# A transformer trunk on one core: 1 / rms broadcast by two transfers instead of matmuls in three stages, and two steps of the weight splitting moved

## The chip, the cores and the metric

The kernel runs on one core of a Trainium2 chip. The metric is the device time of one execution in microseconds. "Before" is the kernel as it stood, "after" the kernel with the change. A core has five engines with instruction queues of their own, which run in order: PE (TensorE, matmuls), DVE (VectorE), ACT (ScalarE), POOL (GpSimd) and SP (which here only issues transfers). PEld is the loading of weights into TensorE.

## The reference

Two layers over 256 tokens of width 1024, all in float32:

```python
for i in range(DEPTH):                                   # DEPTH = 2
    h = h + 0.5 * swiglu(rms_norm(h, ffn_norm[i, 0]), ffn_w_in[i, 0], ffn_w_out[i, 0])
    u = rms_norm(h, mix_norm[i])
    h = h + (mla_mixer(u, ...) if i == 0 else fox_mixer(u, ...))
    h = h + 0.5 * swiglu(rms_norm(h, ffn_norm[i, 1]), ffn_w_in[i, 1], ffn_w_out[i, 1])
    gate = jax.nn.sigmoid(rms_norm(h, ple_norm[i]) @ ple_w_gate[i])
    h = h + gate * (p[i] @ ple_w_proj[i])
return rms_norm(h, final_norm)

def rms_norm(x, g):  return x * lax.rsqrt(jnp.mean(x * x, axis=-1) + 1e-6) * g
def swiglu(x, w_in, w_out):
    gate, up = jnp.split(x @ w_in, 2, axis=-1)           # 1024 -> 2 x 2816
    return (jax.nn.silu(gate) * up) @ w_out
```

`mla_mixer` is low-rank attention with 8 heads and a rotary key, `fox_mixer` attention with 8 heads and a forget gate. There are four feed-forward stages; I call them first to fourth. The second and fourth follow MLA and FoX.

## The kernel before, in words

The activations stand transposed: 128 features on the partitions, 256 tokens along the free axis, in eight blocks (`state`, `hT`). Every float32 matmul is made of float32r parts: an operand is split into a high part and the rest. A weight block comes from memory as `raw` (SP's queue, four buffers), ScalarE writes its high part `whi` (line 101), VectorE the rest `wlo` (line 105), into one of seven pairs of buffers. `W.pump()` puts one `wlo`, and up to two `whi` ahead of it, into the queues at the place where it is called; `W.begin()` puts one `whi` alone. The order of the program text is the order of the queues (`manual_schedule`): no scheduler moves anything.

A `Norm` collects a stage's squares (`sq`, added up on GpSimd as `acc`). The gain is multiplied into the matmul operand at once, 1 / rms only into the results. For that `by_token` sums `acc` over the partitions with matmuls by a column of ones (`pst`), forms the mean `v` on VectorE and takes the power -0.5 on GpSimd: `rtok`, one number per token, tokens on the partitions. `by_column` turns it round: matmuls against the identity give `pb`, with token t's number in column t of every partition, and ScalarE copies it to `rb`.

A feed-forward stage runs over 22 column blocks c, each a `pg` (gate) and a `pu` (up) of eight blocks of k in a PSUM bank; seven banks rotate. Of each, VectorE makes `two` = bank times `rb` (line 341), GpSimd adds its halves to `gu`, ScalarE applies Silu, GpSimd multiplies to `hid`, ScalarE and VectorE split that into `hs`. The first `two` stands behind the second `pu` in the program, because `rb` is wanted there. Then eight output blocks `po` follow. The first stage is special: it starts with four banks (`first`), while its weights come in, and has its sums from ScalarE (`sums`).

In MLA's attention the program goes over heads h: `shares(h - 2)` (VectorE: `inv`, `pr` scaled), `turn` (TensorE `pt`, ScalarE `ptS`), `scores(h - 1)` (TensorE `psc`, VectorE `pr` and bias `nm`, ScalarE the exponentials with their sums `den`), `values` (TensorE `po`). The weights of the output projection `mla_o` are split on the way: at the heads in `MLA_HIGHS` a `whi`, in `MLA_LOWS` a `wlo`. The rotated queries `yz` go to `kqv` by transfers of SP's queue. FoX first computes v by tokens (`pv`, three column blocks of eight k), and needs `rb` only for the queries and keys after that.

Of the kernel before, what the change touches and what calls it, by code (L numbers as in the profile page):

```python
# [11 lines left out]
F32 = mybir.dt.float32  # L12
# [3 lines left out]
AF = mybir.ActivationFunctionType  # L16
# [3 lines left out]
P = 128  # L20
D = 1024
T = 256
# [22 lines left out]

MLA_FILLS = {(6, 1): 3, (7, 1): 4, (8, 0): 1, (8, 1): 5, (9, 0): 4, (9, 1): 3, (10, 0): 2, (10, 1): 2}

MLA_HIGHS, MLA_LOWS = (0, 1, 6, 7, 8), (0, 1, 3, 6, 7, 8)
FOX_FILLS = {(8, 0): 4, (8, 1): 7, (9, 0): 6, (9, 1): 5}

PI_IN = 3.1415925
# [93 lines left out]
def trunk(ctx, tc, xT, xt, pT, pos, freq, bf, lead0, lead1, ffn_in, ffn_out, w_down, w_uq, w_ukv, mla_o,  # L145
          fox_qk, fox_v, fox_o, ple_gate, ple_proj, ple_rows, gain_row, out):
    nc = tc.nc
# [3 lines left out]
    act = ctx.enter_context(tc.tile_pool(name="act", bufs=2))  # L151
    work = ctx.enter_context(tc.tile_pool(name="work", bufs=2))
    psum = ctx.enter_context(tc.tile_pool(name="psum", bufs=7, space=bass.MemoryType.PSUM))
    psm = ctx.enter_context(tc.tile_pool(name="psm", bufs=1, space=bass.MemoryType.PSUM))


# [63 lines left out]
    W = Weights(nc, wp, plan)  # L220
# [52 lines left out]
    class Norm:  # L273
# [50 lines left out]
        def by_column(self):  # L324
            pb = psm.tile([P, T], F32, name="pb", tag="small")
            for t in range(2):
                nc.tensor.matmul(pb[:, t * P:(t + 1) * P], self.rtok[:, t:t + 1].to_broadcast([P, P]), ident,
                                 start=True, stop=True)
            self.rb = work.tile([P, T], F32, name="rb", bufs=3)
            nc.scalar.activation(self.rb, pb, AF.Copy)  # L330
            self.rb2 = self.rb.rearrange("p (o t) -> p o t", o=1).to_broadcast([P, 2, T])


    def ffn(norm, nxt, then=None, first=None, meanwhile=None, later=None):
        hs = big.tile([P, KF, 2, T], F32R, name="hs", tag="big")
        meanwhile = meanwhile or iter(())
        gu, hid = {}, {}
# [32 lines left out]
        if first:  # L370
            waits.append((bank("pg"), bank("pu")))
            first([p for ps in waits for p in ps])
        else:
            blocks(waits[0], norm.pair)
            W.pump(2)
        at = len(waits)
        for c in range(at, KF):
            pg = bank("pg")
            block(pg, norm.pair)
            if c == at:  # L380
                if not first:
                    norm.by_token()
                W.pump()
            else:
                gate(c, pg)
            pu = bank("pu")
            block(pu, norm.pair)
            if c == at:
                norm.by_column()
                for x, ps in enumerate(waits):  # L390
                    gate(x, ps[0], x)
                    up(x, ps[1], 0)
                gate(c, pg)
            up(c, pu, c > at)
# [304 lines left out]
    def fox(norm, nxt):  # L699
# [50 lines left out]
        for c in range(3):  # L750
            pv = [bank("pv0", (P, FV)), bank("pv1", (P, FV))]
            for k in range(KD):
                if k % 3 == 0:
                    w, = W.get()
                a = (k % 3) * FV
                for t in range(2):
                    mm3(pv[t], [norm.pair[:, k, u, t * P:(t + 1) * P] for u in range(2)],
                        [u[:, a:a + FV] for u in w[1:]], k == 0, k == KD - 1)
                if (c, k) == (0, 5):
                    norm.by_token()  # L760
                elif (c, k) == (1, 0):
                    norm.by_column()
                elif (c, k) == (1, 4):
                    steps = gates()
                if steps:
                    next(steps, None)
                if k % 3 == 2 or k == KD - 1:
                    W.done(w)
                    W.pump()
                    if k == 2:  # L770
                        W.catch_up(5)
            b = 0 if c else H
            for t in range(2):
                r = norm.rtok[:, t:t + 1]
                if c == 0:
                    nc.scalar.activation(zt[:, t, :].rearrange("p (j i) -> p j i", i=32)[:, :, :H],
                                         pv[t][:, :H].rearrange("p (o h) -> p o h", o=1).to_broadcast([P, 3, H]),
                                         AF.Copy, scale=r)
                nc.scalar.activation(v[:, t, c * FV + b - H:(c + 1) * FV - H], pv[t][:, b:], AF.Copy, scale=r)
# [223 lines left out]
    def first(ps):  # L1003
# [6 lines left out]
        for k in range(1, KD):  # L1010
            if k % 2 == 0:
                w, = W.get()
            for i, p in enumerate(ps):
                part(p, w, n0.pair, range(k, k + 1), KD - 1, at=lambda x: (k % 2 * 4 + i) * P)
            if k % 2:
                W.done(w)
                W.pump()
            if k == 1:

                n0.sums = const.tile([P, 2], F32, name="sums")  # L1020
                for t in range(2):
                    nc.scalar.activation(tokens[:, t, :], tokens[:, t, :], AF.Square,
                                         accum_out=n0.sums[:, t:t + 1])
            if k == 5:
                n0.by_token()


# [114 lines left out]
    for i in range(2):  # L1142
# [8 lines left out]
        if i == 0:  # L1151
            n0, n1 = Norm(G_FFN + 16, KD, D), Norm(G_MIX + 8, KD, D)
            ple(p.pair, n3, n0)
            ffn(n0, n1, AF.Exp)
        else:
            ple_by_token(p.pair, n3)

# [83 lines left out]
```

## Time and profile before

| | |
|---|---|
| median of 3 runs | 995.11 us (994.88 to 996.27) |
| the profiled execution's own time | 997.11 us |
| its span from first to last instruction | 995.3 us |
| mean granted TensorE clock | 0.998 |
| DMA | 182.26 MB, 183 GB/s, 58.4% of 16 engines' span on SP's queue |

A row of the timeline is start, duration in us, engine, line, operation, output <- inputs and shape; in brackets the idle time before it and whose work ended it. A row with xN stands for N in a row. A row of a list of waits is "engine, tile, line <- engine, tile, line: us in total, times, longest". Places in the span: MLA from about 194 to 263 us, the second feed-forward stage from 264, FoX from about 668 to 771, the fourth feed-forward stage from 771.5.

### The profile page before, as it was taken

How to read it: one execution, taken by the hardware profiler on the slowest of the kernel's cores; microseconds unless marked ns; L12 is line 12 of the kernel's file. 1: busy time of each engine (PE TensorE's matmuls, PEld its weight loads, DVE VectorE, ACT ScalarE, POOL GpSimd, SP SyncE). 2: the span in 40 equal slices, each digit the busy share in tenths (PEclk: the TensorE clock that was granted, in tenths of full speed). 3: DMA queues.
4: the chain of work that ended last, by engine and by line, in shares of the span. 5: the costliest groups of instructions: out<-in, count | busy, mean ns of one | idle time of the engine just before them, and what ended most of it. 6: DMA issues, size and time to landing. Idle time of an engine off the chain costs nothing.

```text
span 995.3 us, 15921 instructions
## 1 busy us (share of the span) xinstructions
PE 984.1 (99%) x5850; PEld 869.3 (87%) x5850; DVE 741.2 (74%) x1089; ACT 515.3 (52%) x820; POOL 425.8 (43%) x348
## 2 busy tenths in 40 slices
PE   8999999999999999999999999999999999999996
PEld 7888888998988888889988888899889888888885
DVE  6777879677877887667878886666877778786664
ACT  7555544456555454545555544537445554444552
POOL 1777731110277765111477673211221577771110
PEclk9999999999999999999999999999999999999999
DMA  8676666563356666665466665656543566666561
GB/s 314 181 253 210 195 173 198 183 182 115 115 185 209 191 189 176 190 202 185 142 200 208 191 186 175 193 178 219 153 148 100 179 209 194 189 179 204 180 208 42
DMA packets 53405, 182.26 MB, mean 183 GB/s; under 512 B 6224, under 2 KB 7760, under 8 KB 53200
## 3 DMA queue, kind: packets, MB, share of 16 engines
q1 hardware_dynamic: 52752, 180.40, 58.4%
q8 instruction: 46, 0.75, 0.3%
q10 hardware_dynamic: 576, 0.85, 0.3%
q14 instruction: 31, 0.25, 0.1%
HBM read 179.00 MB, written 1.05 MB: 181 GB/s over the span
## 4 chain that ended last, share of the span: by engine, by line
PE 94%; DMA 2%; DVE 1%; ACT 1%; issue 1%; POOL 0%; SPq 0%; POOLq 0%; ACTq 0%; DVEq 0%
PE po L247 16%; PE pu L247 16%; PE pg L247 16%; PE po L248 8%; PE pu L248 8%; PE pg L248 8%; PE ps L247 5%; PE ps L248 2%; PE ps L234 2%; PE ps L233 2%; PE ps L232 2%; DMA raw<-in_ffn_in_dram 1%; PE pv L232 1%; PE pv L234 1%; PE pv L233 1%; DMA lead<-in_lead_dram 1%
## 5 line engine op out<-in xcount | busy, mean ns | idle before, releaser
L105 DVE TENSOR_TENSOR wlo<-raw,whi 128x1024 fp32r<-128x1024 f32 (+2 forms) x339 | 416.6, 1237 | 15.2 <-ACT whi L101 14.7
L101 ACT ACTIVATE whi<-raw 128x1024 fp32r<-128x1024 f32 (+2 forms) x339 | 335.3, 1022 | 26.5 <-DMA raw<-in_ffn_in_dram 14.2
L343 POOL TENSOR_TENSOR gu<-two 128x256 f32<-128x256 f32 x176 | 235.7, 1340 | 118.0 <-DVE two L341 108.5
L247 PE MATMUL pg<-u,whi 128*128 128x512 f32 x702 | 251.2, 395 | 0.4 <-ACT whi L997 0.4
L247 PE MATMUL pu<-u,whi 128*128 128x512 f32 x702 | 251.0, 395 | 0.0
L247 PE MATMUL po<-hs,whi 128*128 128x512 f32 x704 | 246.8, 394 | 0.0
L248 PE MATMUL pg<-u,wlo 128*128 128x256 f32 x702 | 197.0, 281 | 0.3 <-DVE wlo L228 0.3
L248 PE MATMUL po<-hs,wlo 128*128 128x256 f32 x704 | 197.2, 280 | 0.0
L248 PE MATMUL pu<-u,wlo 128*128 128x256 f32 x702 | 196.8, 280 | 0.0
L247 PEld LDWEIGHTS po<-hs,whi 128*128 128x128 f32 x704 | 132.2, 188 | 31.3
L247 PEld LDWEIGHTS pg<-u,whi 128*128 128x128 f32 x702 | 131.8, 188 | 31.5 <-ACT whi L997 0.7
L247 PEld LDWEIGHTS pu<-u,whi 128*128 128x128 f32 x702 | 131.8, 188 | 30.9
L248 PEld LDWEIGHTS pg<-u,wlo 128*128 128x128 f32 x702 | 132.1, 188 | 1.0 <-DVE wlo L228 1.0
L248 PEld LDWEIGHTS po<-hs,wlo 128*128 128x128 f32 x704 | 132.3, 188 | 0.0
L248 PEld LDWEIGHTS pu<-u,wlo 128*128 128x128 f32 x702 | 132.1, 188 | 0.0
L303 POOL TENSOR_TENSOR acc<-acc,sq 128x256 f32<-128x256 f32 x42 | 46.3, 1102 | 174.2 <-ACT sq L298 152.7
L224 ACT ACTIVATE hs<-hid 128x256 fp32r<-128x256 f32 x88 | 36.8, 418 | 143.6 <-POOL hid L361 141.5
L361 POOL TENSOR_TENSOR hid<-sg,gu 128x256 f32<-128x256 f32 x88 | 105.5, 1199 | 6.9
L228 DVE TENSOR_TENSOR hs<-hid,hs 128x256 fp32r<-128x256 f32 x88 | 63.4, 720 | 48.7 <-ACT hs L224 48.7
L341 DVE TENSOR_TENSOR two<-pg,rb 128x512 f32<-128x512 f32 x88 | 60.3, 685 | 47.9 <-PE pg L248 39.9
L287 ACT ACTIVATE u<-state 128x256 fp32r<-128x256 f32 x47 | 24.0, 510 | 123.5 <-DVE state L408 105.3
L355 ACT ACTIVATE sg<-gu 128x256 f32<-128x256 f32 x88 | 36.8, 418 | 79.3 <-POOL gu L343 79.3
(258 smaller groups left out, 1163.4 us busy)
## 6 DMA issues: line engine op xcount, KB each, us to landing
raw<-in_ffn_in_dram SPq DMA_DIRECT2D x172, 512.0 KB, 4.1
raw<-in_ffn_out_dram SPq DMA_DIRECT2D x64, 512.0 KB, 3.8
raw<-in_ffn_out_dram SPq DMA_DIRECT2D x32, 384.0 KB, 3.4
raw<-in_fox_qk_dram SPq DMA_DIRECT2D x16, 512.0 KB, 4.6
raw<-in_mla_o_dram SPq DMA_DIRECT2D x8, 512.0 KB, 4.7
raw<-in_ple_gate_dram SPq DMA_DIRECT2D x8, 512.0 KB, 4.9
raw<-in_fox_o_dram SPq DMA_DIRECT2D x8, 512.0 KB, 3.5
raw<-in_ple_rows_dram SPq DMA_DIRECT2D x8, 512.0 KB, 4.5
```

The source lines that it names most:

```text
L101: self.nc.scalar.activation(self.pairs[i][0][:, c], self.raws[i][:, c], AF.Copy)
L105: self.nc.vector.tensor_sub(lo[:, c], self.raws[i][:, c], hi[:, c].bitcast(F32))
L224: nc.scalar.activation(hi, src, AF.Copy)
L228: nc.vector.tensor_sub(lo, src, hi.bitcast(F32))
L232: nc.tensor.matmul(ps, w[0], x[0], start=first, stop=False)
L247: nc.tensor.matmul(ps, hi, x[:, k], start=k == 0, stop=False)
L248: nc.tensor.matmul(ps[:, 1, :], lo, x[:, k, 0, :], start=False, stop=k == last)
L303: nc.gpsimd.tensor_add(new, self.acc, sq)
L341: nc.vector.tensor_mul(two, ps, norm.rb2)
L343: nc.gpsimd.tensor_add(gu[c, i], two[:, 0, :], two[:, 1, :])
L355: nc.scalar.activation(sg, gu.pop((c, 0)), AF.Silu)
L361: nc.gpsimd.tensor_mul(hid[c], gu.pop((c, 0)), gu.pop((c, 1)))
```

## The change

In the second and fourth feed-forward stage (`soon=True`) and in FoX's projections, `by_column` is replaced by `spread`: a transfer from GpSimd's queue writes the 256 values of `rtok` to a row in memory (`row`), and a second one, which waits for the first, reads that row into all 128 partitions of `rb`. In the two feed-forward stages `by_token` moves from behind the second `pg` to behind the first `pg` and `pu`, with one `wlo` moved behind it. In the third stage nothing changes (`soon=False`). In the first, `by_token` comes one step of k earlier. In MLA one `whi` moves from head 1 to head 2 and one `wlo` from head 3 to head 2. The whole diff:

```diff
--- before.py
+++ after.py
@@ -45,7 +45,7 @@
 
 MLA_FILLS = {(6, 1): 3, (7, 1): 4, (8, 0): 1, (8, 1): 5, (9, 0): 4, (9, 1): 3, (10, 0): 2, (10, 1): 2}
 
-MLA_HIGHS, MLA_LOWS = (0, 1, 6, 7, 8), (0, 1, 3, 6, 7, 8)
+MLA_HIGHS, MLA_LOWS = (0, 2, 6, 7, 8), (0, 1, 2, 6, 7, 8)
 FOX_FILLS = {(8, 0): 4, (8, 1): 7, (9, 0): 6, (9, 1): 5}
 
 PI_IN = 3.1415925
@@ -151,6 +151,7 @@
     act = ctx.enter_context(tc.tile_pool(name="act", bufs=2))
     work = ctx.enter_context(tc.tile_pool(name="work", bufs=2))
     psum = ctx.enter_context(tc.tile_pool(name="psum", bufs=7, space=bass.MemoryType.PSUM))
+    dram = ctx.enter_context(tc.tile_pool(name="dram", bufs=1, space=bass.MemoryType.DRAM))
     psm = ctx.enter_context(tc.tile_pool(name="psm", bufs=1, space=bass.MemoryType.PSUM))
 
 
@@ -328,10 +329,21 @@
                                  start=True, stop=True)
             self.rb = work.tile([P, T], F32, name="rb", bufs=3)
             nc.scalar.activation(self.rb, pb, AF.Copy)
+            self.both()
+
+        def spread(self):
+
+            row = dram.tile([1, T], F32, name="row", bufs=4)
+            nc.gpsimd.dma_start(row.rearrange("o (t p) -> p (o t)", p=P), self.rtok)
+            self.rb = work.tile([P, T], F32, name="rb", bufs=3)
+            nc.gpsimd.dma_start(self.rb, row.to_broadcast([P, T]))
+            self.both()
+
+        def both(self):
             self.rb2 = self.rb.rearrange("p (o t) -> p o t", o=1).to_broadcast([P, 2, T])
 
 
-    def ffn(norm, nxt, then=None, first=None, meanwhile=None, later=None):
+    def ffn(norm, nxt, then=None, first=None, meanwhile=None, later=None, soon=True):
         hs = big.tile([P, KF, 2, T], F32R, name="hs", tag="big")
         meanwhile = meanwhile or iter(())
         gu, hid = {}, {}
@@ -372,13 +384,17 @@
             first([p for ps in waits for p in ps])
         else:
             blocks(waits[0], norm.pair)
-            W.pump(2)
+            W.pump()
+            if soon:
+                norm.by_token()
+                norm.spread()
+            W.pump()
         at = len(waits)
         for c in range(at, KF):
             pg = bank("pg")
             block(pg, norm.pair)
             if c == at:
-                if not first:
+                if not (first or soon):
                     norm.by_token()
                 W.pump()
             else:
@@ -386,7 +402,8 @@
             pu = bank("pu")
             block(pu, norm.pair)
             if c == at:
-                norm.by_column()
+                if first or not soon:
+                    norm.by_column()
                 for x, ps in enumerate(waits):
                     gate(x, ps[0], x)
                     up(x, ps[1], 0)
@@ -758,8 +775,8 @@
                         [u[:, a:a + FV] for u in w[1:]], k == 0, k == KD - 1)
                 if (c, k) == (0, 5):
                     norm.by_token()
-                elif (c, k) == (1, 0):
-                    norm.by_column()
+                elif (c, k) == (0, 7):
+                    norm.spread()
                 elif (c, k) == (1, 4):
                     steps = gates()
                 if steps:
@@ -1021,7 +1038,7 @@
                 for t in range(2):
                     nc.scalar.activation(tokens[:, t, :], tokens[:, t, :], AF.Square,
                                          accum_out=n0.sums[:, t:t + 1])
-            if k == 5:
+            if k == 4:
                 n0.by_token()
 
 
@@ -1151,7 +1168,7 @@
         if i == 0:
             n0, n1 = Norm(G_FFN + 16, KD, D), Norm(G_MIX + 8, KD, D)
             ple(p.pair, n3, n0)
-            ffn(n0, n1, AF.Exp)
+            ffn(n0, n1, AF.Exp, soon=False)
         else:
             ple_by_token(p.pair, n3)
```

VectorE where the second feed-forward stage begins. Before (`u` is the normed operand of the stage, its last block):

```order
L292 SCALAR_TENSOR_TENSOR u<-state,u 128x256
L105 TENSOR_TENSOR wlo<-raw,whi 128x1024 x4
L320 TENSOR_SCALAR v<-pst 128x2
L105 TENSOR_TENSOR wlo<-raw,whi 128x1024
L341 TENSOR_TENSOR two<-pg,rb 128x512
L341 TENSOR_TENSOR two<-pu,rb 128x512
L341 TENSOR_TENSOR two<-pg,rb 128x512
```

and after:

```order
L293 SCALAR_TENSOR_TENSOR u<-state,u 128x256
L105 TENSOR_TENSOR wlo<-raw,whi 128x1024 x3
L321 TENSOR_SCALAR v<-pst 128x2
L105 TENSOR_TENSOR wlo<-raw,whi 128x1024 x2
L353 TENSOR_TENSOR two<-pg,rb 128x512
L353 TENSOR_TENSOR two<-pu,rb 128x512
L353 TENSOR_TENSOR two<-pg,rb 128x512
```

`v` now stands behind three `wlo` and not four. The queue is the same in the fourth stage.

GpSimd at the same place, before:

```order
L322 TENSOR_TENSOR rtok<-v,mhalf 128x2 x2
L303 TENSOR_TENSOR acc<-sq 128x256
L303 TENSOR_TENSOR acc<-acc,sq 128x256 x6
L322 TENSOR_TENSOR rtok<-v,mhalf 128x2
L343 TENSOR_TENSOR gu<-two 128x256 x2
L361 TENSOR_TENSOR hid<-sg,gu 128x256
```

and after:

```order
L323 TENSOR_TENSOR rtok<-v,mhalf 128x2 x2
L304 TENSOR_TENSOR acc<-sq 128x256
L304 TENSOR_TENSOR acc<-acc,sq 128x256 x6
L323 TENSOR_TENSOR rtok<-v,mhalf 128x2
L337 DMA row<-rtok 128x2x1
L339 DMA rb<-row 128x256
L355 TENSOR_TENSOR gu<-two 128x256 x2
L373 TENSOR_TENSOR hid<-sg,gu 128x256
```

The two transfers stand between the power and the first addition, which needs `rb` through `two`.

ScalarE in MLA, where the softmax of the first heads begins (`kqv` holds queries, keys and values), before:

```order
L618 ACTIVATE kqv<-ps 128x512
L101 ACTIVATE whi<-raw 128x1024 x2
L454 ACTIVATE pr,den<-pr,nm,qscale 128x128
L455 ACTIVATE pr,den<-pr,nm,qscale 128x256
L618 ACTIVATE kqv<-ps 128x512
L454 ACTIVATE pr,den<-pr,nm,qscale 128x128
L455 ACTIVATE pr,den<-pr,nm,qscale 128x256
```

and after:

```order
L635 ACTIVATE kqv<-ps 128x512
L101 ACTIVATE whi<-raw 128x1024
L471 ACTIVATE pr,den<-pr,nm,qscale 128x128
L472 ACTIVATE pr,den<-pr,nm,qscale 128x256
L635 ACTIVATE kqv<-ps 128x512
L101 ACTIVATE whi<-raw 128x1024
L471 ACTIVATE pr,den<-pr,nm,qscale 128x128
```

One `whi` has moved behind the exponentials of head 0 and the copy of queries.

## Prediction

> **What bounds the kernel now.** I read the page's busy shares first, then who waited for whom on TensorE, then the timelines of the places that the change touches.
>
> ```profile
> PE 984.1 (99%) x5850; PEld 869.3 (87%) x5850; DVE 741.2 (74%) x1089; ACT 515.3 (52%) x820; POOL 425.8 (43%) x348
> PE pb L327 <- POOL rtok L322: 1.0, 1, 1.0
> PE pt L469 <- DVE pr L462: 0.5, 1, 0.5
> PE po L476 <- ACT ptS L471: 0.3, 1, 0.3
> ```
>
> The first row is the page's: TensorE is busy 984.1 of 995.3 us, so it is the bound, and no other engine is above 74%. The others are from the waits of PE (us in total, times, longest). Apart from waits of a few tenths at the very start, these three are all it ever waits for. So the time falls by what TensorE is spared, and by these waits if they go; it rises by any new wait on TensorE. Nothing else counts.
>
> **Part 1: the broadcast matmuls, three stages.** In the second and fourth feed-forward stage and in the FoX projections, `by_column` (matmuls `pb`, then a copy on ScalarE) goes. TensorE's timeline in the second feed-forward stage:
>
> ```profile
> 275.35 0.28 PE L248 MATMUL pu<-u,wlo 128*128 128x256 f32 x1
> 275.47 0.60 PE L327 MATMUL pb<-ident,rtok 128*128 128x128 f32 x4
> 275.83 0.48 PE L247 MATMUL pg<-u,whi 128*128 128x512 f32 x1
> ```
>
> Matmuls overlap, so the cost is from start to start: `pb` holds the stream from 275.47 to 275.83, 0.36 us. Three times that is 1.1 us off the bound engine. The `pst` matmuls move but stay. ScalarE loses a 0.39 us copy per stage, which the bound does not feel.
>
> **Part 2: the first stage, `by_token` one step earlier.**
>
> ```profile
> 18.06 0.19 ACT L1022 ACTIVATION_READ_ACCUMULATOR lead<-lead 128x1 f32 x1
> 21.00 1.22 DVE L105 TENSOR_TENSOR wlo<-raw,whi 128x1024 fp32r<-128x1024 f32 x1 [4.07 <-ACT whi L101]
> 22.14 0.16 DVE L320 TENSOR_SCALAR v<-sums 128x2 f32<-128x2 f32 x1
> 22.46 1.69 POOL L322 TENSOR_TENSOR rtok<-v,mhalf 128x2 f32<-128x2 f32 x1 [20.97 <-DVE v L320]
> 22.93 0.28 PE L248 MATMUL pu<-u,wlo 128*128 128x256 f32 x1
> 24.20 0.71 PE L327 MATMUL pb<-ident,rtok 128*128 128x128 f32 x4 [1.00 <-POOL rtok L322]
> 23.75 1.06 ACT L101 ACTIVATE whi<-raw 128x1024 fp32r<-128x1024 f32 x1 [0.19 <-DMA raw<-in_ffn_in_dram]
> 39.07 1.21 DVE L105 TENSOR_TENSOR wlo<-raw,whi 128x1024 fp32r<-128x1024 f32 x1
> 41.58 0.39 PE L247 MATMUL pg<-u,whi 128*128 128x512 f32 x1
> ```
>
> The sums are ready at 18.25, but `v` stands on VectorE behind a weight subtraction that waits for its data until 21.00. With `v` ahead of it the power ends near 20.2, long before TensorE wants `pb` at 23.05 (22.93 plus the 0.12 between starts). The idle time from 23.05 to 24.20, 1.15 us, goes. What is late next: the copy `rb` stays behind the `whi` that ends at 24.81 on ScalarE, so the scaled evacuations don't move, while TensorE is 1.15 earlier. The tightest weight behind them, by my pairing of the subtractions with the plan, is the one that ends at 40.28, wanted at 41.58 and then at 40.43: 0.15 to spare. I take 1.1, between 0 and 1.15.
>
> **Part 3: `MLA_HIGHS` and `MLA_LOWS`.** One `whi` and one `wlo` of w_o change places with softmax work.
>
> ```profile
> 219.11 0.16 DVE L446 SCALAR_TENSOR_TENSOR nm<-m,qscale 128x2 f32<-128x2 f32 x1
> 219.58 1.06 ACT L101 ACTIVATE whi<-raw 128x1024 fp32r<-128x1024 f32 x1 [0.87 <-DMA raw<-in_mla_o_dram]
> 219.79 1.22 DVE L105 TENSOR_TENSOR wlo<-raw,whi 128x1024 fp32r<-128x1024 f32 x1
> 221.73 0.17 DVE L461 RECIPROCAL inv<-den 128x2 f32<-128x2 f32 x1 [0.72 <-ACT pr L455]
> 222.36 0.30 PE L469 MATMUL pt<-ident,pr 128*128 128x128 f32 x1 [0.54 <-DVE pr L462]
> 224.47 0.17 DVE L461 RECIPROCAL inv<-den 128x2 f32<-128x2 f32 x1 [1.24 <-ACT pr L455]
> 226.48 1.21 DVE L105 TENSOR_TENSOR wlo<-raw,whi 128x1024 fp32r<-128x1024 f32 x1
> 231.39 0.48 PE L476 MATMUL po<-ptS,kqv 128*128 128x256 f32 x1 [0.27 <-ACT ptS L471]
> ```
>
> The exponentials of head 0 have their bias at 219.27 but stand behind a `whi` that waits for its transfer and ends at 220.6. With the `whi` behind them they start 1.2 us earlier; the reciprocal then starts when VectorE's `wlo` ends, 220.95 instead of 221.73, and 0.78 covers the 0.54 of `pt`. The `wlo` of 226.48 moves up into the gap of 1.24 us before 224.47, so heads 2 and 3 come up to 1.2 earlier, which covers the 0.27 of `po`. Its raw transfer is issued sooner and stands on SP's queue ahead of the last four rotary copies, which are not ready yet then. Bounds 0 and 0.81; I take 0.7.
>
> **Part 4: what the transfers cost.** In FoX `rtok` is there at 673.2 and VectorE first uses `rb` at 691.87: 18 us, ample for any price below. In the feed-forward stages it is tight:
>
> ```profile
> 671.54 1.63 POOL L322 TENSOR_TENSOR rtok<-v,mhalf 128x2 f32<-128x2 f32 x1 [3.41 <-DVE v L320]
> 691.87 0.69 DVE L787 TENSOR_TENSOR two<-ps,rb 128x512 f32<-128x512 f32 x1 [0.36 <-PE ps L248]
> 266.13 0.88 POOL L303 TENSOR_TENSOR acc<-acc,sq 128x256 f32<-128x256 f32 x1 [0.39 <-ACT sq L298]
> 266.32 5.17 DVE L105 TENSOR_TENSOR wlo<-raw,whi 128x1024 fp32r<-128x1024 f32 x4
> 269.29 0.28 PE L248 MATMUL pu<-u,wlo 128*128 128x256 f32 x1
> 272.99 1.67 POOL L322 TENSOR_TENSOR rtok<-v,mhalf 128x2 f32<-128x2 f32 x1 [5.98 <-DVE v L320]
> 276.53 0.69 DVE L341 TENSOR_TENSOR two<-pg,rb 128x512 f32<-128x512 f32 x1 [2.43 <-ACT rb L330]
> 286.07 1.21 DVE L105 TENSOR_TENSOR wlo<-raw,whi 128x1024 fp32r<-128x1024 f32 x1
> 289.92 0.39 PE L247 MATMUL pu<-u,whi 128*128 128x512 f32 x1
> 784.25 0.69 DVE L341 TENSOR_TENSOR two<-pg,rb 128x512 f32<-128x512 f32 x1 [2.38 <-ACT rb L330]
> 793.77 1.21 DVE L105 TENSOR_TENSOR wlo<-raw,whi 128x1024 fp32r<-128x1024 f32 x1
> 797.62 0.39 PE L247 MATMUL pu<-u,whi 128*128 128x512 f32 x1
> ```
>
> Start. The sum of squares ends at 267.0, before `pst` at 269.41, so TensorE doesn't wait for it. After three of the four `wlo` VectorE is at 270.2 and does `v`. In the row of before the power ended 2 us after its `v` began, so `rtok` is there near 272.1. The two transfers follow; call the time from there to the first `two` the chain.
>
> Deadline. While VectorE waits for `rb`, every later `wlo` stands behind it. By the pairing, the tightest is the one that ends at 287.28, 10.75 after the first `two`, wanted at 289.92 less the 0.36 of `pb`: 289.56. So `rb` may come by 278.7 (0.1 for the hand-over), 2.2 later than now: the chain may last 6.6 us. In the fourth stage the same sum (793.77 + 1.21 - 784.25 = 10.73; 797.26) gives 6.5. Beyond that TensorE idles in both stages by the excess. PSUM isn't the limit: three free banks last past 283.9.
>
> Price. Nothing in this trace uses GpSimd's queue. The nearest rows (KB each, us to landing):
>
> ```profile
> fr<-in_freq_dram SPq DMA_DIRECT2D x1, 0.5 KB, 3.2
> pos_i<-in_pos_dram SPq DMA_DIRECT2D x1, 128.0 KB, 4.2
> p_sb<-in_pT_dram ACTq DMA_DIRECT2D x2, 256.0 KB, 2.6
> out_dram<-fin SPq DMA_DIRECT2D x2, 256.0 KB, 2.4
> ```
>
> `fr` is 128 single words, like `row`'s 256; `pos_i` has exactly `rb`'s shape, but stood in SP's queue among weights; `p_sb` had a queue of its own while weights streamed, as `rb` will. I take 3.2 for `row`, 2.6 for `rb`, 0.1 for each of two waits: 6.0, no stall. Low end: 2.4 + 2.6 = 5.0. High end: 3.2 + 4.2, and for GpSimd's own work per transfer its slowest power, 1.7 each: 10.8.
>
> The Trainium skill, "DMA: Bandwidth & Descriptors", section "Anatomy of one DMA — SWDGE (gpsimd) path", prices a transfer from this queue at about 2.0 us plus bytes over 436 GB/s; by it the chain would be an estimated 4.3 us and there would be no stall. No run here shows it yet.
>
> Behind the transfers on GpSimd stand only the additions that need `rb` anyway. The weight stream is hardly touched: 129 KB per stage against 0.5 MB per weight.
>
> **The sum.** 1.1 + 1.1 + 0.7 + 0 = 2.9 us. The profiled span is 995.3 of its execution's 997.1 us; against it the sum gives a span of 992.4. The median of the runs is 995.1, so 992.2. What a measurement of this kernel can tell from no change is about 0.2%, 2.0 us.
>
> **Rivals.**
>
> (a) The chain is too long by a little. Between 7 and 9 us it eats (chain - 6.5) twice: at 8 us, 3.0 of the 2.9, and the time is 995.2. For it speaks that `row` is words of four bytes and that the landings above vary from 2.4 to 4.2.
>
> (b) Slower: GpSimd writes the description of 256 separate words slowly. Then `rb` is late in two stages and each further microsecond costs two. No gain is left at 8.0; slower beyond 0.2% begins at 9.0. At the high end of 10.8 it is 4.3 x 2 - 2.9 = +5.7: 1000.8. For it: the power, a tiny job, takes 1.7 us on this engine beside VectorE. Against: VectorE is idle during most of the chain, and the engine is otherwise free.
>
> A milder form is that VectorE locks GpSimd out: if descriptors had to wait for the last `wlo`, which ends near 272.7, the chain would grow by 0.6 to 6.6, costing 0.1 in all: 992.3. The Trainium skill, "SBUF — State Buffer", section "Who interferes with whom", says that a tensor-tensor operation with both inputs in SBUF holds off GpSimd's reads, but not, as it infers, descriptor generation.
>
> (c) Parts 2 and 3 don't arrive: other waits take over at the same places (0.15 to spare in part 2). With nothing of both it is 1.1 alone: 994.0.
>
> **How the numbers follow.** Forecast, chain up to 7: 0.62, times from 991.5 to 993.1. (a) 0.20, 993.1 to 997.1. (b) 0.11, above. (c) 0.07, 993.2 to 994.5. Faster by over 0.2% (below 993.1) is the forecast: 0.62; same is (a) and (c): 0.27; slower 0.11. The range is 991.4 to 996.0: it leaves out (b), the last quarter of (a), and little below.
>
> **What would show it.** The first feed-forward stage without the 1.0 wait of `pb`; no wait of `pt` and `po` on PE; 20 instead of 32 `pb` matmul passes; `two` starting near 278 in the second stage (less what came earlier); PE without waits on `wlo` at the fourth `pu`. Such a wait near 288 and 795, with `two` waiting for the transfer of `rb`, proves me wrong.

## The result and the profile after

After takes 1009.63 us (median of 4 runs, 1009.17 to 1010.53), before, timed beside it, 995.37 (994.88 to 996.27). The ratio is 1.0142, 95% interval 1.0129 to 1.0154: 1.4% slower. The forecast was 992.2, in a range of 991.4 to 996.0.

The profiled execution of after took 1010.53 us, with a span of 1008.8. First the busy shares from its page, then the longest waits of PE behind the very start (us in total, times, longest):

```profile
PE 987.4 (98%) x5838; PEld 871.4 (86%) x5838; DVE 735.6 (73%) x1089; ACT 514.5 (51%) x817; POOL 427.9 (42%) x354
```

```profile
PE pu L248 <- DVE two L353: 7.8, 2, 4.5
PE pu L249 <- DVE wlo L105: 3.7, 2, 2.0
PE pst L318 <- POOL acc L304: 0.8, 1, 0.8
```

The waits of `pb` and `pt` are gone. In their place stand two pairs of new ones, 11.5 us together, one pair in each of the two feed-forward stages. The wait of `pst` (0.8) lies near 973 and also came up in `i_forms2` below, which is before with unread transfers, so the change does not explain it. The timelines of GpSimd, VectorE and TensorE in the second stage, one after the other, and then in the fourth:

```profile
267.78 1.61 POOL L323 TENSOR_TENSOR rtok<-v,mhalf 128x2 f32<-128x2 f32 x1 [3.50 <-DVE v L321]
269.70 0.90 POOL L337 DMA_DIRECT2D row<-rtok  x1 [0.31 <-POOL rtok L323]
280.38 0.59 POOL L339 DMA_DIRECT2D rb<-row  x1 [9.78 <-DMA row<-rtok]
283.60 0.69 DVE L353 TENSOR_TENSOR two<-pg,rb 128x512 f32<-128x512 f32 x1 [12.27 <-DMA rb<-row]
284.44 0.48 PE L248 MATMUL pu<-u,whi 128*128 128x512 f32 x1 [3.21 <-DVE two L353]
286.93 0.58 PE L249 MATMUL pu<-u,wlo 128*128 128x256 f32 x1 [2.01 <-DVE wlo L105]
...
782.38 1.63 POOL L323 TENSOR_TENSOR rtok<-v,mhalf 128x2 f32<-128x2 f32 x1 [3.50 <-DVE v L321]
784.30 0.74 POOL L337 DMA_DIRECT2D row<-rtok  x1 [0.29 <-POOL rtok L323]
794.98 0.57 POOL L339 DMA_DIRECT2D rb<-row  x1 [9.94 <-DMA row<-rtok]
799.56 0.69 DVE L353 TENSOR_TENSOR two<-pg,rb 128x512 f32<-128x512 f32 x1 [13.69 <-DMA rb<-row]
800.40 0.77 PE L248 MATMUL pu<-u,whi 128*128 128x512 f32 x1 [4.55 <-DVE two L353]
802.89 0.58 PE L249 MATMUL pu<-u,wlo 128*128 128x256 f32 x1 [1.73 <-DVE wlo L105]
```

Read it down. The power ends at 269.39 and the first `two` starts at 283.60: the chain lasts 14.2 us, not 6.0. Of it 10.4 us lie between the issue of `row` and its landing; GpSimd itself is occupied for only 0.90. In the fourth stage the chain is 15.6 us. At 281.2 the banks of PSUM are used up, and TensorE stands until the first `two` has freed one; soon after it stands again, for a `wlo` that is behind the late `two` on VectorE.

The list of DMA issues (KB each, median us to landing):

```profile
row<-rtok POOLq DMA_DIRECT2D x3, 1.0 KB, 10.4
rb<-row POOLq DMA_DIRECT2D x3, 128.0 KB, 4.5
```

So 1 KB takes over three times the 3.2 us of `fr`, the row from which it was priced. And the idle time is not all. Windows of 4 us (busy time by engine, then the granted clock, the DMA share, GB/s):

```profile
280.00:284.00 4.00, 1.23 (x8) 0.82 (x6) 0.40 (x1) 0.00 (x0) 0.59 (x1) 1.00 0.16 33
284.00:288.00 4.00, 1.55 (x5) 1.17 (x6) 2.93 (x5) 1.78 (x3) 3.55 (x4) 0.60 0.05 6
288.00:292.00 4.00, 4.00 (x15) 3.37 (x15) 2.99 (x4) 1.75 (x3) 2.89 (x4) 0.55 0.36 125
292.00:296.00 4.00, 4.00 (x25) 3.50 (x24) 3.94 (x5) 2.35 (x4) 2.90 (x3) 1.00 0.56 162
```

After the wait the granted clock is near one half in the two windows: TensorE is busy for all of 288 to 292 and issues 15 matmuls, against 25 in the next window. The trace's record of the clock has 0.5 for 6.83 us here, from 284.8, and again in the fourth stage from 800.2; before had no such stretch before its last microseconds. The Trainium skill, "TensorE: Matmul & The Clock Gate", section "Part 1: The HAM clock gate (the "warmup" mystery)", says that the array falls to half its clock after an idle window of about 3.4 us. The trace agrees roughly: of the 3.41 us ahead of the two stretches TensorE stood idle for 3.08 and for all; `m_quads` below shows that 2.15 can be enough.

### The profile page after: what moved, and what is told of

Read it like the earlier page. It is cut to its first block, busy times and chain, and to the rows that moved or that the text cites. A ratio compares the mean times of both kernels' runs of the same rounds, so it can differ in the third digit from the quotient of the medians.

```text
span 1008.8 us, 15918 instructions
## 1 busy us (share of the span) xinstructions
PE 987.4 (98%) x5838; PEld 871.4 (86%) x5838; DVE 735.6 (73%) x1089; ACT 514.5 (51%) x817; POOL 427.9 (42%) x354
## 4 chain that ended last, share of the span: by engine, by line
PE 90%; DVE 4%; DMA 3%; issue 1%; ACT 1%; POOL 1%; POOLq 0%; SPq 0%; DVEq 0%; ACTq 0%
PE po L248 16%; PE pu L248 15%; PE pg L248 15%; PE po L249 8%; PE pu L249 8%; PE pg L249 8%; PE ps L248 4%; PE ps L249 2%; DMA row<-rtok 2%; PE ps L233 2%; PE ps L234 2%; PE ps L235 2%; DVE wlo L105 1%; DVE state L534 1%; DMA rb<-row 1%
## 5 line engine op out<-in xcount | busy, mean ns | idle before, releaser
L355 POOL TENSOR_TENSOR gu<-two 128x256 f32<-128x256 f32 x176 | 225.8, 1284 | 120.6 <-DVE two L353 110.9
L248 PE MATMUL pu<-u,whi 128*128 128x512 f32 x702 | 254.9, 399 | 7.8 <-DVE two L353 7.8
L249 PE MATMUL pu<-u,wlo 128*128 128x256 f32 x702 | 198.9, 283 | 3.7 <-DVE wlo L105 3.7
L373 POOL TENSOR_TENSOR hid<-sg,gu 128x256 f32<-128x256 f32 x88 | 114.2, 1298 | 6.9
L229 DVE TENSOR_TENSOR hs<-hid,hs 128x256 fp32r<-128x256 f32 x88 | 58.8, 668 | 59.4 <-ACT hs L225 59.4
```

The lines of the kernel that those rows point to most:

```text
L229: nc.vector.tensor_sub(lo, src, hi.bitcast(F32))
L248: nc.tensor.matmul(ps, hi, x[:, k], start=k == 0, stop=False)
L249: nc.tensor.matmul(ps[:, 1, :], lo, x[:, k, 0, :], start=False, stop=k == last)
L355: nc.gpsimd.tensor_add(gu[c, i], two[:, 0, :], two[:, 1, :])
L373: nc.gpsimd.tensor_mul(hid[c], gu.pop((c, 0)), gu.pop((c, 1)))
```

## The experiments

Twelve kernels were run. Each time the kernel before was timed beside them; "before" in brackets is its median there.

**Is it the chain, and what is the rest worth?** `a_no_spread` and `b_fox_spread` take the transfers out of all three stages, or out of the two feed-forward stages only:

```diff
-    def ffn(..., later=None, soon=True):
+    def ffn(..., later=None, soon=False):
# a_no_spread also:
-                elif (c, k) == (0, 7):
-                    norm.spread()
+                elif (c, k) == (1, 0):
+                    norm.by_column()
```

> After with every broadcast back on TensorE at before's places: only parts 2 and 3 of the prediction are left (the sums of the first feed-forward stage at k = 4, the moved halves of v and w_o). By the prediction's terms 1.1 + 0.7 = 1.8 us faster than before, about 993.5. Rival (the clock's and the waits' loss comes from those two parts too, or their gain is taken back later): not faster than 995.

> After with the spread by transfers in the FoX stage only. If the transfers' chain is hidden there and only the 0.36 us of the two broadcast matmuls goes: 0.4 us faster than the kernel with no spread, about 993.1. Rival (the chain is too long there as well): slower than the kernel with no spread by 0.5 us or more.

`a_no_spread`: 994.53 us (before 994.93, ratio 0.9994, 0.9985 to 1.0003). `b_fox_spread`: 993.76, ratio 0.9986, 0.9978 to 0.9995. So the loss comes with the transfers in the two feed-forward stages alone. FoX's transfers are hidden: in after `rb` is asked for at 688.10 and lands at 694.20, and VectorE first uses it at 696.42, without a wait that the trace names: of the 18 us of cover 2.2 were left.

```profile
696.42 0.69 DVE L804 TENSOR_TENSOR two<-ps,rb 128x512 f32<-128x512 f32 x1
```

Against `a_no_spread`, FoX's transfers gain 0.8 us by the medians, where 0.36 was expected. Parts 2 and 3 brought 0.4 and not 1.8, and the interval includes no gain at all. `c_token_only` looks at part 2 alone:

```diff
-            if k == 5:
+            if k == 4:
                 n0.by_token()
```

> Before with part 2 alone, the sums of the first feed-forward stage at k = 4 and not 5. By the prediction's term: 1.1 us faster, 0.9989. Rival (the 1.0 us wait for the power was in the one profiled execution only, where the power took 1.69 us; in two later traces of the same code it took 0.71 and TensorE did not wait): no change, 0.9995 to 1.0005.

995.29 us (before 995.49, ratio 0.9998, 0.9989 to 1.0007): the rival, though the 0.9989 that was forecast is the very edge of the interval. The wait belongs to some executions only. In the profiled one of before the power took 1.69 us; in `h_forms` below, whose program is before's up to this place, it took 0.71, and TensorE did not wait for it:

```profile
20.83 0.71 POOL L326 TENSOR_TENSOR rtok<-v,mhalf 128x2 f32<-128x2 f32 x1 [19.33 <-DVE v L324]
```

In another trace of the same code (`l_forms3`) it took 1.70, and the 1.0 us wait was there again; of four such traces two have it. The wait of `pt` differs from run to run too: 0.54 in before, none in `c_token_only`, whose MLA is before's. From the `pst` ahead of MLA's attention to that of the second stage it is 60.1 us in `c_token_only` and 59.6 in `a_no_spread`, so part 3 is worth about 0.5.

**Are the small writes themselves the harm, or the waiting?** `j_unread` issues `row` where after does, but nobody reads it; the broadcast is made on TensorE:

```diff
             nc.gpsimd.dma_start(row.rearrange("o (t p) -> p (o t)", p=P), self.rtok)
-            self.rb = work.tile([P, T], F32, name="rb", bufs=3)
-            nc.gpsimd.dma_start(self.rb, row.to_broadcast([P, T]))
# and norm.by_column() again at before's places
```

> After with the word transfers `row` issued where after issues them, but not read: the broadcast in the three stages is made on TensorE as before. Nobody waits for `row`. If all of the loss is the waiting for the chain: as the kernel with no spread, 994.5 (at the same time of before, 994.9). Rival (the small writes hold up the weights' transfers on the same engines, as the stretch of 0 GB/s behind them suggests): TensorE waits for weights in the second or fourth stage or FoX, and the time is 997 or more.

994.45 us (before 995.23, ratio 0.9991, 0.9982 to 1.0001), no wait of TensorE for weights, with `row` landing after 10.0 to 11.1 us: at these places the writes harm nobody. The loss is the waiting.

`k_no_row` keeps the transfer `rb` and drops `row`; it reads the first 256 gains in place of 1 / rms, so its results are not the reference's, but the work is the same:

```diff
-            row = dram.tile([1, T], F32, name="row", bufs=4)
-            nc.gpsimd.dma_start(row.rearrange("o (t p) -> p (o t)", p=P), self.rtok)
-            nc.gpsimd.dma_start(self.rb, row.to_broadcast([P, T]))
+            nc.gpsimd.dma_start(self.rb, gain_row[:, :T].to_broadcast([P, T]))
```

> After without the word transfer: `rb` is read from the first 256 values of `gain_row` in memory, behind the power in GpSimd's program, so that the chain holds one transfer and not two (the values are not 1 / rms). By the prediction's terms the chain is then about 0.2 + 2.6 to 6.1 us, inside the 6.5 us, and the two stages gain 0.36 us each over the kernel with FoX's spread alone: about 993.0 (before 994.9). Rival (transfers of GpSimd's queue cost something apart from the row's landing, or `rb` alone is late): TensorE still idles for `two` in one of the stages, 995 or more.

992.88 us, ratio 0.9974, 0.9965 to 0.9984, and TensorE does not wait for `two` or `wlo` in these stages. Its second stage:

```profile
268.25 1.61 POOL L323 TENSOR_TENSOR rtok<-v,mhalf 128x2 f32<-128x2 f32 x1 [3.50 <-DVE v L321]
275.25 0.69 DVE L351 TENSOR_TENSOR two<-pg,rb 128x512 f32<-128x512 f32 x1 [3.39 <-DMA rb<-in_gain_row_dram]
```

The chain is 5.4 us, 5.6 in the fourth stage. With a chain inside its limit the kernel lands where the prediction put it. The price of `row` is what is left, and this kernel gives it a scale. The start of `pst` and of the `pg` of block 4 (blocks counted from 0), in `k_no_row` and then in after, second stage and fourth:

```profile
267.16 0.50 PE L318 MATMUL pst<-ones,acc 128*128 128x1 f32 x4
284.44 0.40 PE L248 MATMUL pg<-u,whi 128*128 128x512 f32 x1
...
773.99 0.50 PE L318 MATMUL pst<-ones,acc 128*128 128x1 f32 x4
791.27 0.39 PE L248 MATMUL pg<-u,whi 128*128 128x512 f32 x1
```

```profile
266.60 0.50 PE L318 MATMUL pst<-ones,acc 128*128 128x1 f32 x4
291.71 0.40 PE L248 MATMUL pg<-u,whi 128*128 128x512 f32 x1
...
781.22 0.50 PE L318 MATMUL pst<-ones,acc 128*128 128x1 f32 x4
807.42 0.39 PE L248 MATMUL pg<-u,whi 128*128 128x512 f32 x1
```

17.28 us in both stages of `k_no_row`, 25.11 and 26.20 in after: 7.8 and 8.9 us lost, 16.7 together. That is the whole distance between the two kernels, 1.0142 - 0.9974 = 1.68% of 995, 16.7 us. The trace names 5.2 and 6.3 of it as idle time; the remaining 2.6 in each stage is lost while the clock is at one half. Whether it would be saved at the whole clock is asked below.

**Where does the idle time begin?** `o_delay` is `k_no_row` with work on GpSimd ahead of `rb`:

```diff
+            for _ in range(4):
+                late = work.tile([P, T], F32, name="late", bufs=1)
+                nc.gpsimd.tensor_add(late, self.acc, self.acc)
```

> The kernel without a word transfer (`rb` read from `gain_row`, values not 1 / rms; chain 5.4 us, 0.9974 of before), with four additions of 128x256 on GpSimd (0.73 to 1.6 us each) ahead of `rb`: the chain becomes 8.3 to 11.8 us, with nothing else changed on the engines that do the work. It shows where idle time begins. By the prediction's limit TensorE idles for all beyond 6.5 us: 1.8 to 5.3 us per stage, 996.5 to 1004. If only the bank limits (11.0 us): 992.5 to 994.5.

993.78 us (before 995.5, ratio 0.9981, 0.9972 to 0.9990). Its timelines of GpSimd, VectorE and TensorE in the second stage:

```profile
269.60 3.77 POOL L338 TENSOR_TENSOR late<-acc 128x256 f32<-128x256 f32 x4
276.84 0.69 DVE L354 TENSOR_TENSOR two<-pg,rb 128x512 f32<-128x512 f32 x1 [5.31 <-DMA rb<-in_gain_row_dram]
287.65 0.39 PE L249 MATMUL pu<-u,wlo 128*128 128x256 f32 x1 [0.20 <-DVE wlo L105]
```

The additions were short (3.8 us for four), so the chain came to 7.2 us only, 7.0 in the fourth stage, below what was expected; `rb` landed in 3.5. It is the useful place. The trace names 0.20 us of idle time, on a `wlo`, in the second stage and none in the fourth. But it counts from the modelled end of the matmul before, 0.39 us after that one's start, and undisturbed the next one starts after 0.23. The same `pu` in the fourth stage:

```profile
794.28 0.40 PE L248 MATMUL pu<-u,whi 128*128 128x512 f32 x1
794.81 0.39 PE L249 MATMUL pu<-u,wlo 128*128 128x256 f32 x1
```

From start to start it is 0.53 and not 0.23: 0.30 us are lost here and 0.37 in the second stage (287.05 to 287.65). So the limit is about 6.8 and 6.7 us; the prediction had 6.6 and 6.5. The bank's limit of about 11 us, where the first `two` comes too late for a free bank (14.2 - 3.2 in after), is not the first one.

**Why does `row` take 10 us?** `h_forms`, `i_forms2` and `l_forms3` are the kernel before with other transfers of `rtok` behind the powers, which nobody reads:

```diff
             nc.gpsimd.tensor_tensor(self.rtok, v, mhalf, op=ALU.pow)
+            # by the place in the program, one of
+            q.dma_start(row.rearrange("o (t p) -> p (o t)", p=P), self.rtok)       # words side by side
+            q.dma_start(row.rearrange("o (p t) -> p (o t)", p=P), self.rtok)       # 128 pieces of 8 bytes
+            q.dma_start(row.rearrange("(t p) k -> p t k", p=P)[:, :, 0], self.rtok)  # words 4 k bytes apart
+            q.dma_start(row, ident[:, :n])                                         # 128 pieces of 4 n bytes
+            q.dma_start(on_chip, pos.rearrange("o (t p) -> p (o t)", p=P))         # 256 words read
```

> The kernel before, with extra transfers whose result nobody reads, one behind each of nine powers: (1) the 256 separate words of `rtok` to memory by GpSimd's queue, as after does it; (2) the same 1 KB with each partition's two words side by side, 128 pieces of 8 bytes; (3) one column, 128 words; (4) eight partitions, 8 pieces of 8 bytes; (5) 256 separate words read from memory by GpSimd's queue; (6) as 1 by SP's queue; (7) as 1 by ScalarE's queue; (8) as 1 again; (9) as 5 by SP's queue. Theory W (each separate word has its price, 10.4 us for 256): 1, 8, 6, 7, 5 and 9 take about 10, 2 and 3 about 6, 4 about 3. Rival Q (GpSimd's queue has a high fixed price): 1 to 5 and 8 all take 9 to 10.4, and 6, 7 and 9 about 3, like `fr`. Rival M (words written to memory are slow, words read are not): 1, 6, 7 and 8 take about 10, and 5 and 9 about 3. The time itself stays within 1 us of before, since nobody waits.

> The kernel before with other transfers that nobody reads: (1) 128 pieces of 512 bytes to memory by GpSimd's queue; (2) the 256 words, but each to a line of its own, 512 bytes apart; (3) 128 pieces of 64 bytes; (4) `rtok` to another tile on the chip, 128 pieces of 8 bytes; (5) as 1 by SP's queue; (6) 128 pieces of 16 bytes; (7) as 2 by SP's queue; (8) the 256 words side by side as after has them. Theory S (a piece much smaller than 512 bytes is slow to write to memory): 1 and 5 about 3, as `out_dram` (2.5) and `p_sb` (2.7) are; 2, 3, 6, 7 and 8 all 7.5 to 10.4; 4 about 3. Rival L (many words that fall into the same short line of memory wait for each other): 2 and 7 about 3 to 5, 1 and 5 about 3, 3 about 4, 6 and 8 about 8. Rival N (the number of pieces alone, wherever they go): 1, 3, 4, 5 and 6 all about 8.

> The kernel before with further transfers to memory that nobody reads, all by GpSimd's queue: the 256 words of `rtok` 64, 16, 32, 8, and 128 bytes apart, 16 again, 128 pieces of 8 bytes side by side, and 128 single words side by side. Theory L (words that fall into the same short line of memory wait for each other; 256 words side by side took 9.0 to 10.7, words 512 bytes apart 2.3): the landing falls with the distance, about 2.3 to 3 at 128 and 64, 3 to 3.5 at 32, 4 to 5 at 16 and 6 at 8 bytes; 128 pieces of 8 bytes about 6 to 8. Rival (the landing depends on the place in the program, on what else is under way, and the 2.3 was luck): no order by distance, some of the wide ones at 8 or more.

The landings, one number per transfer (queue GpSimd's unless named):

| form | us from issue to landing |
|---|---|
| 256 words side by side, 1 KB | 8.8, 10.4, 9.3; SP's queue 8.2; ScalarE's 10.2; in the kernels that transfer it as after does 8.8 to 11.1 |
| 128 words side by side | 8.3, 9.1 |
| 128 pieces of 8 bytes side by side | 7.8, 5.5 |
| 8 pieces of 8 bytes | 3.6 |
| 128 pieces of 16, 64, 512 bytes side by side | 4.4, 4.1, 4.0 (512 by SP's queue: 4.7) |
| 256 words 8, 16, 32, 64, 128 bytes apart | 6.1; 2.5 and 5.8; 4.0; 5.0; 4.0 |
| 256 words 512 bytes apart | 2.3; SP's queue 4.3 |
| 128 pieces of 8 bytes, on the chip only | 3.5 |
| 256 words read from memory | 5.6; SP's queue 5.1 |

Of these, from the lists of DMA issues in `h_forms` (the first row is GpSimd's three, a median over two word transfers and the 8-byte pieces) and, for windows around one issue each, in `i_forms2` at 199.9 (512 bytes apart), 671 (16 bytes) and 963 (side by side):

```profile
row<-rtok POOLq DMA_DIRECT2D x3, 1.0 KB, 8.8
row<-rtok SPq DMA_DIRECT2D x1, 1.0 KB, 8.2
row<-rtok ACTq DMA_DIRECT2D x1, 1.0 KB, 10.2
row<-in_pos_dram POOLq DMA_DIRECT2D x1, 1.0 KB, 5.6
```

```profile
row<-rtok POOLq DMA_DIRECT2D x1, 1.0 KB, 2.3
...
row<-ident POOLq DMA_DIRECT2D x1, 2.0 KB, 4.4
...
row<-rtok POOLq DMA_DIRECT2D x1, 1.0 KB, 9.3
```

The queue isn't it: SP's and ScalarE's are as slow. The number of words isn't it: the same 256 words from the same tile take 2.3 us when each has 512 bytes of memory to itself, 8.8 at the same place in the program side by side. Nor is a small piece slow by itself. Slow are words and 8-byte pieces written side by side: the theory that neighbours in a short line of memory wait for each other (L) fits best, but it is argued and not shown. Of the others expected above W, Q, S and N are out; M holds only for words side by side, and the reads took more than its 3 us. A strict order by distance they don't show: 16 bytes apart landed in 2.5 at one place and in 5.8 at another, and 64 bytes apart, at the busy start, in 5.0; pieces of 16 bytes side by side landed in 4.4, where L expected about 8. How long a line is, and where in the memory's path they wait, stays open.

`h_forms` had a surprise: it took 1002.16 us (one run; before 994.93). Nobody waits for its transfers, but three of them (256 words, 128 pieces of 8 bytes, 128 words) follow each other between 200 and 220, in MLA. Issues between 195 and 226 us, in `h_forms` and in before:

```profile
raw<-in_mla_o_dram SPq DMA_DIRECT2D x6, 512.0 KB, 8.5
kqv<-yz SPq DMA_DIRECT2D x12, 64.0 KB, 7.9
```

```profile
raw<-in_mla_o_dram SPq DMA_DIRECT2D x7, 512.0 KB, 4.7
kqv<-yz SPq DMA_DIRECT2D x12, 64.0 KB, 3.8
```

The weights and the rotary copies land twice as late while the words are written and just after, and TensorE then waits 5.9 us for `pr`, with 6.83 us of half clock from 223.6. `i_forms2` and `l_forms3`, with one transfer of words there, 512 and 16 bytes apart, took 996.94 and 998.13 (one run each; before 995.23 and 995.49).

**Does a shorter `row` bring the idle time down?** `m_quads` writes each token's pair twice, 16 bytes per partition, reads 2 KB into every partition and lets `two` take its columns in steps of four; `n_dense` first copies those columns to a dense `rb`:

```diff
+                wide = lambda x: x.rearrange("p (o t) -> p o t", o=1).to_broadcast([P, 2, 2])
+                nc.gpsimd.tensor_tensor(self.rtok.rearrange(...), wide(v), wide(mhalf), op=ALU.pow)
+            row = dram.tile([P, 4], F32, name="row4", bufs=4)
+            nc.gpsimd.dma_start(row, self.rtok)
+            rb = work.tile([P, P, 4], F32, name="rb4", bufs=1)
+            nc.gpsimd.dma_start(rb.rearrange("q p j -> q (p j)"), ...to_broadcast([P, 4 * P]))
# n_dense:
+            nc.gpsimd.tensor_copy(self.rb.rearrange("q (j p) -> q j p", j=2), rb.rearrange("q p j -> q j p")[:, :2])
```

> After with another `row` in the second and the fourth feed-forward stage: the power writes each token's pair twice, so that 128 pieces of 16 bytes go to memory (2 KB, landing 4.4 us in a run of before that nobody waited for) and 256 KB come back, each partition's pair of columns in steps of four; FoX as in after. By theory L `row` lands in about 4.4 and not 10.4, and the chain is 0.2 + 4.4 + about 4 to 6 = 9 to 10.5 us. If TensorE idles from 6.5 us on, as the prediction has it: 2.5 to 4 us in each stage, 998 to 1001. If the true limit is the bank that the first `two` frees (in after 14.2 - 3.2 = 11.0 us): no idle for `two`, at most 1 us for the late `wlo`, and 993 to 995 (before 994.9 to 995.4). Rival (the landing has nothing to do with the size of the pieces): as after, 1009.

> The kernel with pieces of 16 bytes, but GpSimd copies the needed columns of what came back to a dense `rb` (one copy of 128x256, about 0.8 us), so that every `two` reads side by side again and takes 0.68 us, not 1.08. The chain is about 8.1 + 0.8 to 9.2 + 0.8, 9 to 10 us. By the prediction's limit (idle for all beyond 6.5 us): 2.5 and 3.5 us of idle, about 999. If the first limit is the bank at 11.0 us and what is lost sooner is only the late `wlo` behind the late `two`: 0.5 to 1.5 us in each stage, 994 to 996. In both cases no wait of `po` for `hs`. Rival (the 11 us of the strided kernel were the transfers and not its strided reads): 1005 or more.

`row` landed in 4.1 and 4.9, as expected, and the chain of `m_quads` is 8.1 and 9.2 us. Yet it took 1009.79 us (before 995.49, ratio 1.0149, 1.0134 to 1.0165): a miss, though not for the rival's reason. Its `two` takes 1.08 us instead of 0.68, and TensorE then waits for VectorE at the start of both stages and again where their output blocks begin, 2.15 us each. The first `two` of the second stage, and the waits of PE:

```profile
277.87 1.08 DVE L366 TENSOR_TENSOR two<-pg,rb 128x512 f32<-128x512 f32 x1 [6.45 <-DMA rb<-row]
```

```profile
PE po L248 <- DVE hs L229: 4.3, 2, 2.2
PE pu L249 <- DVE wlo L105: 3.6, 4, 1.8
PE pg L249 <- DVE wlo L105: 3.2, 2, 1.6
```

`n_dense` has no such strided reads and no wait for `hs`; it took 999.02 us (before 995.5, ratio 1.0034, 1.0021 to 1.0048), about what the prediction's limit gives. Its waits of PE, and the first `two` of the second stage:

```profile
PE pg L249 <- DVE wlo L105: 2.2, 2, 1.1
PE pu L249 <- DVE wlo L105: 1.6, 4, 0.8
```

```profile
278.86 0.69 DVE L366 TENSOR_TENSOR two<-pg,rb 128x512 f32<-128x512 f32 x1 [7.36 <-POOL rb L352]
```

Its chains are 8.9 and 9.2 us, its idle time 1.7 and 2.1, 3.8 together, all on `wlo`. The time is 6.0 us above `k_no_row`'s. The waits named are less than that, for the reason given above; from start to start 5.4 are found in these stages (table below).

**Is the half clock due to the idle time?** `g_busy` puts matmuls that nobody reads where after stands still:

```diff
+            if c == 3 and soon and not first:
+                idle = psm.tile([P, 2, T], F32, name="idle", tag="small")
+                for _ in range(24):
+                    nc.tensor.matmul(idle, norm.pair[:, 0, 0, :P], norm.pair[:, 0], start=True, stop=True)
             pu = bank("pu")
```

> After, with 24 matmuls of 512 columns into a bank that nobody reads ahead of the fourth `pu` of the second and of the fourth feed-forward stage: 24 x 0.223 = 5.35 us of work in the place where TensorE stood idle for 5.2 and 6.3 us. Theory (the clock falls to half because TensorE stood idle): no 0.5 in the clock's record of these stages, 2 x 3.4 us come back, and the time is about 1003. Rival (the clock falls for another reason, and the idle time is all that TensorE loses): 1009 to 1010.

In its windows the clock stays whole:

```profile
284.00:288.00 4.00, 4.00 (x20) 3.28 (x19) 3.30 (x4) 1.37 (x2) 2.81 (x3) 1.00 0.02 4
288.00:292.00 4.00, 3.10 (x18) 2.45 (x17) 3.07 (x4) 1.78 (x3) 2.89 (x4) 1.00 0.43 131
```

So the half clock follows the idle time. But the time was 1008.79 (before 994.93, ratio 1.0138, 1.0123 to 1.0154), not 1003. The traces say why. From `pst` to the start of the `pg` of block 5, one block further than above, `k_no_row` takes 22.9 us in both stages. The others (second stage, fourth stage, us):

| kernel | chain | `pst` to `pg` of block 5 | more than `k_no_row` | clock |
|---|---|---|---|---|
| `o_delay` | 7.2, 7.0 | 23.4, 23.3 | 0.5, 0.4 | whole |
| `n_dense` | 8.9, 9.2 | 25.3, 25.8 | 2.5, 2.9 | whole |
| `g_busy` | 13.9, 13.0 | 30.1, 29.2 | 7.2, 6.3 | whole |
| after | 14.2, 15.6 | 30.7, 31.8 | 7.9, 8.9 | half for 6.83 each |

In all of them the loss is the chain less 6.3 to 6.7 us, whether the clock falls or not. At the whole clock TensorE only comes sooner to the next late `wlo` and waits there. In the list of waits `g_busy` has

```profile
PE pg L249 <- DVE wlo L105: 0.9, 1, 0.9
```

in the second stage, where after has no wait. So the cause of the half clock is shown, and as far as these traces show its price here is next to nothing: at most 0.3 us beyond what the chain explains in the second stage of after, none in the fourth. Beyond about 6.6 us a microsecond of chain is a microsecond of TensorE. Of the 3.3 us that `g_busy` gains on after in this table, 2.9 are its shorter chains. By the medians it gains 0.8; how long the chains of the executions without a trace were is not known.

## Why the prediction was wrong

- **Part 4, the price of `row`.** This is the step that failed: "I take 3.2 for `row`". It measured 10.4, 9.5 and 10.4. `fr`, the nearest row, reads 128 words from memory into partitions; `row` writes 256 words side by side into memory, and no row of the trace did that. Even a read of 256 words took 5.1 to 5.6. The high end of 10.8 us for the chain also came from `fr`, so it was no bound: the chain was 14.2 and 15.6.
- **Part 4, the price of `rb`.** 2.6 was taken, 3.2 to 6.1 measured; the high end of 4.2 was too low as well. This would have mattered too. After's chains with `row` at 3.2 would have been 7.0 and 8.4 us (14.2 - 7.2, 15.6 - 7.2), 0.4 and 1.9 beyond the limit that was forecast: 2.3 of the 2.9 us, which is rival (a). `k_no_row` has no stall because it has one transfer and not two.
- **Part 4, the deadline.** Right: 6.6 and 6.5, measured 6.8 and 6.7 in `o_delay`, on the `wlo` named. The rule "TensorE idles in both stages by the excess" gives (14.2 - 6.6) + (15.6 - 6.5) = 16.7 us for the true chains, and 16.7 to 16.8 were lost. That is not luck: by the same rule `g_busy` loses 13.8 and `n_dense` 5.0, and 13.5 and 5.4 were measured. What the prediction did not have, the full banks and the half clock, changes where the time is lost, and its amount hardly at all.
- **PSUM.** "The limit isn't PSUM" held for the chains that were considered. At 14.2 us the banks run out before the late `wlo` is wanted, and the first wait shows as one for `two`.
- **Part 1.** Right: 20 `pb` passes instead of 32. From the first `pg` of the second stage to FoX's first `pv` it is 401.27 us in `a_no_spread` and 400.87 in `k_no_row`, 0.40 less where 0.36 was taken. By the medians `k_no_row` and `b_fox_spread` differ by 0.12%, 1.2 us, for two stages (0.7 expected, inside the intervals).
- **Part 2.** 1.1 was taken from one execution; it is 0.2 us, uncertain by 0.9. The wait does go, but in two of four traces of before's code it isn't there.
- **Part 3.** 0.7 taken, about 0.5 by the traces; 0.4 for parts 2 and 3 together by the medians.
- **The sum without a stall** of 2.9 us stands against 0.26% of 995, 2.6 us, in `k_no_row` (0.16 to 0.35%). That is partly luck: by the medians parts 2 and 3 brought 0.4 for 1.8, and the three broadcasts 2.0 for 1.1.
- **The rivals.** (b) named the right consequence, and its line of two microseconds per microsecond of chain leads from 1000.8 at 10.8 to about 1009 at the true chains. Its cause was wrong: GpSimd's part was 0.9 and 0.6 us, and other queues are as slow. It got 0.11 because every price in the trace was that of a different kind of transfer. Its milder form did not come: GpSimd was done with `row` at 270.60, while a `wlo` ran on VectorE from 270.11 to 271.34.
- **A reading.** Of the waits at the very start one is 1.1 us long, not a few tenths. It is the same before and after, so nothing hangs on it.
- **The Trainium skill's price** ("DMA: Bandwidth & Descriptors", section "Anatomy of one DMA — SWDGE (gpsimd) path": about 2.0 us and the bytes' time) holds here for the words that lie 512 bytes apart, 2.3 us, and fails for the same words side by side by some 7 to 9 us.

Of the kernels whose `rb` is 1 / rms, `b_fox_spread` (the moved halves, the earlier sums and FoX's transfers, without the transfers in the feed-forward stages) is the fastest: 0.9986 of before, 0.9978 to 0.9995. It beats both.

## What to carry to other kernels

Price a transfer by a row of the same direction and the same pattern of addresses; if there is none, the range is open upwards, and one unread copy of the transfer in the old kernel measures it. Before a result is sent through memory in single words, ask how the words lie: side by side they cost 8 to 11 us here, and a broadcast that costs the bound engine 0.36 us can't be replaced by that where only 6.6 us of cover exist. Count a loss from start to start, up to a place behind all the late work: named waits can miss part of it, and a slow stretch can stand where a wait would stand otherwise. A wait that stands in one profile is worth its length only if it stands in the others.

## What the runs showed of the hardware that I had not expected

- Writing 256 words side by side to memory: 8.2 to 11.1 us from three different queues; the same words 512 bytes apart: 2.3 and 4.3.
- Around three transfers of words or 8-byte pieces side by side within 12 us others were late, in one run: 512 KB weight blocks landed in 8.5 instead of 4.7 us, 64 KB copies on the chip in 7.9 instead of 3.8.
- In the clock's record of all fourteen traces, every completed stretch at one clock is a whole multiple of 3.413 us long. Cut into such pieces, the clock fell behind each piece in which TensorE was idle for 2.15 us or more (18 pieces, 14 of them at a kernel's end; idle time by the modelled ends), and behind none with 1.77 or less. At half clock it rose behind pieces with at most 0.25 us of idle time and stayed behind those with 1.95 or more. So the place of a wait decides: `m_quads` stood twice for 2.15 us. Near 910 the wait lay in one piece, and 3.41 us of half clock followed; near 396 it lay across two, and none did.
- A multiplication of VectorE on 128x512 float32 with one operand read in steps of 16 bytes took 1.08 us instead of 0.68.
- The power of 128x2 numbers on GpSimd takes 0.71 or 1.6 to 1.7 us in the same place of the same program.
